# A hybrid encoder layer on one core: branch A's first four score tiles set between the last token tiles of its q projection

## The chip, the cores and the metric

The kernel runs on one core of a Trainium2 chip. The metric is device microseconds of one execution. Beside the times there is the trace of one profiled execution. Engines are named as the profile does: PE is TensorE (PEld its weight loads), DVE is VectorE, ACT is ScalarE, POOL is GpSimd, SP is SyncE, which issues nearly all DMAs here.

## The reference

One encoder layer on 1024 tokens of width 1024, in float32. Two attention branches share one projection, are merged by gates, and a squared-ReLU MLP and a gated embedding follow:

```python
h = rmsnorm(x, norm_mix_g[i])
z = h @ w_in[i]
qa, ka, va, qb, kb, vb, ga, gb = jnp.split(z, split_at, axis=-1)
y_a = mixer_a(qa, ka, va, q_norm_g[i], k_norm_g[i], row_ids, col_ids) @ w_out_a[i]
y_b = mixer_b(qb, kb, vb, rel_bias) @ w_out_b[i]
x = x + (gate_a * y_a + gate_b * y_b) @ w_out[i]
x = x + jnp.square(jax.nn.relu(rmsnorm(x, norm_mlp_g[i]) @ w_ff1[i])) @ w_ff2[i]
x = x + sigmoid(rmsnorm(x, norm_ple_g[i]) @ w_ple_gate[i]) * (p[i] @ w_ple[i])
return rmsnorm(x, final_norm_g)
```

Branch A (`mixer_a`) is dense attention of 8 q heads on 2 k/v heads of width 128. q and k are RMS-normed per head and turned by a rotary table; the softmax runs over all 1024 keys.

## The kernel before, in words

Every float32 product is made of three products of rounded halves: `split` writes `hi` (ACT, L235) and `lo = src - hi` (DVE, L236), and `mm3` (all its matmuls at L239) multiplies hi by hi, hi by lo and lo by hi. Memory is handed out by regions (`Region`), stacks that grow from the left and the right end of SBUF. When a region is closed, a later one may take its addresses, and the framework then sets the waits that this needs. Within the two `tc.manual_schedule` blocks PE runs in program order. Everything else, and the order on ACT, DVE, POOL and SP, is put in order by the framework's scheduler.

The change lies between the stages of branch A:

- `qkv_a` projects k and v (block 0) and q (blocks 1 and 2, four heads each), each block in eight token tiles of 24 matmuls. A tile is squared and summed on ACT (L861) and turned by the rotary table on DVE (L814, L819, L821). Two tiles later PE transposes it (`turn`, L835), ACT copies it out of PSUM (L840) and SP stores it to `qd`. The two last turns of block 2 are left over in `self.turns`. `load_q` brings one q head back and splits it (tile `rq`).
- `attend_a` runs 16 units (head, half of the tokens). A unit has four score tiles (`scores`: 6 matmuls into two PSUM banks, the row maximum on DVE at L926, its product with the row's scale at L928, the exponential on ACT at L930), then 8 key chunks of transposed weights (`weights`: four transposes at L936 and a split, tile `rp`) and their products with v (`values`, 6 matmuls for two chunks). The loop sets the scores of unit u beside the weights and values of unit u-1. `finish` ends a unit: it copies the result (L950), takes reciprocals of the denominators (L952), stores them to DRAM and loads them back as a row spread over all partitions (`rd`, `rb`), multiplies (L957) and splits into `oA` (tile `ro`, L235 and L236).
- `merged_b` (after unit 1's scores are set) splits the merged result of branch B into `oB` (tile `ro` as well).
- `mix_outputs` follows. Its first products need the out-projection's weights, split into the ring `wt` of region `rwt` (8 slots of 1024 words): per column block `wa` (hi, lo) and `wb` (one slot for both).

PSUM has eight banks of 512 words. In `qkv_a` the projection rings over banks 4 to 7, the turns over banks 2 and 3. In `attend_a` the scores take the pairs 0, 1 and 2, 3, the weights' transposes banks 4 to 6, the values bank 7.

The left stack during attention holds, in this order and in words per partition: `kv` 8192, `rq0` 2048, `fp1` 4096, `rq1` 2048, `fp0` 4096, `fp` 3104. Region `fa` (2560: `mix` and the two q rotary tables) is closed when `qkv_a` ends. Afterwards `m` (8192), `rwt` (8192) and `wo` (8192) stand at the same left end.

Of the kernel before, what the change touches and what calls it, by code (L numbers as in the profile page):

```python
# [10 lines left out]
F32 = mybir.dt.float32  # L11
F32R = mybir.dt.float32r
# [8 lines left out]
NT = S // P  # L21
KD = D // P
GRID_W = 64
HA, HKV, DA = 8, 2, 128
# [52 lines left out]
class Ring:  # L77
# [3 lines left out]
    def next(self):  # L81
        s = self.slots[self.i % len(self.slots)]
        self.i += 1
        return s
# [22 lines left out]
def v3(ap, k):  # L107
    return ap.rearrange("p (k c) -> p k c", k=k)
# [117 lines left out]
class Layer:  # L226
# [112 lines left out]
    def mix_inputs(self):  # L339
        tc, nc, io = self.tc, self.nc, self.io  # L340
        rh = Region(tc, "rh", F32R, "right")
        hT = [v3(rh.take(8192), KD) for _ in range(2)]
        wt = rh.ring(N_WT, 1024)
        w_in = io["w_in"][0]
# [239 lines left out]
        self.p_late = [self.fp1.take(1024) for _ in range(4)]  # L584
        halves = [a[:, o:o + 512] for a in self.p_late for o in (0, 512)]
        t_ring, stage = Ring(halves[:6]), Ring(halves[6:])
        fa = Region(tc, "fa", F32, "left")
        mix = fa.take(512)
        tabs = [v3(fa.take(1024), NT) for _ in range(2)] + tabs
        beside = self.merge_b(qk[0], Ring([qk[1][:, :S]] + u_ring.slots))  # L590
        with tc.manual_schedule(engines={mybir.EngineType.PE}):
            self.qkv_a(w_in, wt, hT, tabs, gtmp, t_ring, stage, lambda: self.weights_b(mix), beside)
            fa.close()
            fm.close()
            fq.close()
            rh.close()
            self.attend_a()

    def bias_rows(self, tmp, st, ps):

# [219 lines left out]
                                in1=sin[:, a:a + 32].unsqueeze(1).to_broadcast([P, n, 32]), op=ALU.mult)  # L820
        v.tensor_tensor(out=t1[:, :w], in0=t1[:, :w], in1=t2[:, :w], op=ALU.add)  # L821

    def qkv_a(self, w_in, wt, hT, tabs, gtmp, t_ring, stage, after_kv, beside):

        nc = self.nc
        ps_a, ps_t = Ring(self.bank[4:]), Ring(self.bank[2:4])
        self.ps_w = self.bank[1]
        q_tabs = self.rope_tables("q_norm_g", tabs[:2], gtmp, nc.vector)
        self.turns = []

        def turn(blk, t, t1, n):
            sl = slice(t * P, (t + 1) * P)
            pp = ps_t.next()[:, :n * P]
            for h in range(n):
                nc.tensor.transpose(pp[:, h * P:(h + 1) * P], t1[:, h * P:(h + 1) * P], self.ident)  # L835
            if blk == 0:
                self.split(self.kT[0][:, :, sl], self.kT[1][:, :, sl], v3(pp, 2))
            else:
                st, h0 = stage.next(), (blk - 1) * 4
                nc.scalar.activation(st, pp, AF.Copy)  # L840
                self.load(self.dr["qd"][h0:h0 + 4, :, sl].rearrange("h p t -> p h t"), v3(st, 4))

        for blk in range(3):
            c0 = (C_KA, C_QA, C_QA + 512)[blk]
            w = []
            for kk in range(4):
                w += self.w_rows(w_in, 2 * kk, c0, 512, wt)
            for t in range(NT):
                sl = slice(t * P, (t + 1) * P)
                ps = ps_a.next()  # L850
                for k in range(KD):
                    self.mm3([ps], (hT[0][:, k, sl], hT[1][:, k, sl]), [w[k]], k == 0, k == KD - 1)
                if len(self.turns) == 2:
                    self.turns.pop(0)()
                t1, t2 = t_ring.next(), t_ring.next()
                n = 2 if blk == 0 else 4
                tc_, ts_ = (tabs[2], tabs[3]) if blk == 0 else (tabs[0], tabs[1])
                sm = self.small.next()
                for h in range(n):
                    ss = sm[:, h:h + 1] if blk == 0 else self.q_scale(self.qss, 4 * blk - 4 + h, t)  # L860
                    nc.scalar.activation(t2[:, h * P:(h + 1) * P], ps[:, h * P:(h + 1) * P], AF.Square, accum_out=ss)  # L861
                if blk == 0:
                    self.split(self.vA[0][:, t, :], self.vA[1][:, t, :], ps[:, 256:512])
                self.rope(ps[:, :n * P], n, tc_[:, t, :], ts_[:, t, :], t1, t2)
                if blk == 0:
                    xe, y, tt = sm[:, 2:4], sm[:, 4:6], sm[:, 6:8]
                    nc.vector.tensor_scalar(xe, sm[:, 0:2], 1.0 / DA, EPS, op0=ALU.mult, op1=ALU.add)
                    self.rsqrt(y, xe, tt)
                    for h in range(2):
                        nc.vector.tensor_scalar(t1[:, h * P:(h + 1) * P], t1[:, h * P:(h + 1) * P],  # L870
                                                y[:, h:h + 1], None, op0=ALU.mult)
                self.turns.append(lambda a=(blk, t, t1, n): turn(*a))
                if blk == 0 and t >= NT - 2:
                    next(q_tabs)
                if blk == 1 and t == 2:
                    after_kv()
                if blk == 1 and t >= 4 or blk == 2 and t < 2:
                    next(beside)
                if blk == 2 and t == 3:
                    self.load_q(0)  # L880
            if blk:
                x, r, tt = (a[:, 32 * blk - 32:32 * blk] for a in (self.qss, self.rq, self.qtmp))
                nc.vector.tensor_scalar(x, x, 1.0 / DA, EPS, op0=ALU.mult, op1=ALU.add)
                self.rsqrt(r, x, tt)
                nc.vector.tensor_scalar(r, r, DA ** -0.5, None, op0=ALU.mult)
# [9 lines left out]
        self.split(q[0], q[1], raw)  # L895


    def attend_a(self):
        tc, nc = self.tc, self.nc
        self.ro = Region(tc, "ro", F32R, "right")  # L900
        self.oA = [v3(self.ro.take(8192), HA) for _ in range(2)]
        self.oB = [v3(self.ro.take(2048), 2) for _ in range(2)]
        rp = Region(tc, "rp", F32R, "right")
        pt_ring = rp.ring(6, 1024)
        self.rq_pools.append(Region(tc, "rq1", F32R, "left"))
        self.qr.append([self.rq_pools[1].take(1024) for _ in range(2)])
        f0, fp = (Region(tc, n, F32, "left") for n in ("fp0", "fp"))
        p_ring = Ring([f0.take(1024) for _ in range(4)] + self.p_late)
        ou_ring, rb_ring = fp.ring(3, 512), fp.ring(3, 512)
        den_ring = fp.ring(4, 8)  # L910
        s_ps, t_ps, o_ps = Ring(self.bank2[:2]), Ring(self.bank[4:7]), Ring(self.bank[7:])

        def scores(u, j):
            h, half = divmod(u, 2)
            if half == 0 and j == 0 and h:
                self.load_q(h)
            q = self.qr[h % 2]
            kv = h // (HA // HKV)
            t = half * 4 + j
            sl = slice(t * P, (t + 1) * P)  # L920
            ps = s_ps.next()
            self.mm3([ps[:, 0:512], ps[:, 512:1024]], (q[0][:, sl], q[1][:, sl]),
                     [tuple(self.kT[i][:, kv, c * 512:(c + 1) * 512] for i in range(2)) for c in range(2)],
                     True, True)
            nm = self.small.next()[:, 0:1]
            nc.vector.tensor_reduce(out=nm, in_=ps, axis=AX.X, op=ALU.max, negate=True)  # L926
            r = self.q_scale(self.rq, h, t)
            nc.vector.tensor_tensor(out=nm, in0=nm, in1=r, op=ALU.mult)  # L928
            p = p_ring.next()
            nc.scalar.activation(p, ps, AF.Exp, bias=nm, scale=r, accum_out=dens[u][:, j:j + 1])  # L930
            return p

        def weights(u, probs, kc, o):
            pp = t_ps.next()
            for j in range(4):
                nc.tensor.transpose(pp[:, j * P:(j + 1) * P], probs[j][:, kc * P:(kc + 1) * P], self.ident)  # L936
            pt = pt_ring.next()
            pt = (pt[:, 0:512], pt[:, 512:1024])
            self.split(pt[0], pt[1], pp)
            return u, pt, kc, o  # L940
# [19 lines left out]

        nu = 2 * HA
        dens = {u: None for u in range(nu)}
        probs, late = None, []

        def flush():
            while late:
                args = late.pop(0)
                values(*args)
                if args[2] == NT - 1:
                    finish(args[0], args[3])  # L970

        for u in range(nu + 1):
            nxt = []
            if u < nu:
                dens[u] = den_ring.next()
            for j in range(4):
                if u < nu:
                    nxt.append(scores(u, j))
                if self.turns:
                    self.turns.pop(0)()  # L980
                if u > 0:
                    if j == 0:
                        o = o_ps.next()
                    new = [weights(u - 1, probs, kc, o) for kc in (2 * j, 2 * j + 1)]
                    flush()
                    late += new
            probs = nxt
            if u == 1:
                self.merged_b()
        flush()  # L990
        for region in (rp, fp, f0, self.rq_pools[1], self.fp1, self.rq_pools[0], self.kv):
            region.close()

    def merged_b(self):
# [378 lines left out]
```

## Time and profile before

| | us |
|---|---|
| median of 3 runs | 1803.49 |
| lowest, highest | 1802.71, 1805.03 |
| the profiled execution | 1805.11 |
| its span in the trace | 1803.3 |
| PE busy | 1742.9 |
| DVE busy | 1244.7 |
| ACT busy | 796.4 |

The profiled execution takes 1.8 us more than its span, and 1.62 us more than the median. Times in the trace count from the span's start. `[0.88 <-ACT fp L840]` behind a row means that the engine sat idle for 0.88 us before it and that ACT's instruction at line 840, which handles tile `fp`, ended that. In a row merged from several instructions the second number runs from the first start to the last end. PEclk is the granted clock of TensorE as a share of full speed.

### The profile page before, as it was taken

The page shows a single profiled execution, that of the slowest core. Times are in us where ns is not written, and L with a number is a line of the kernel's source. Part 1 is how long each engine was busy: PE and PEld are TensorE (multiplying, and loading weights), DVE is VectorE, ACT ScalarE, POOL GpSimd, SP SyncE. Part 2 cuts the span into 40 slices and gives each one's busy share as a digit, 9 for nine tenths or more (in the row PEclk, how much of TensorE's full clock was granted, in tenths as well). Part 3 has the DMA queues.
Part 4 walks back from the last instruction along what each step waited for, and adds up shares of the span by engine and source line. Part 5 has one row for each costly group of instructions (what it writes and reads, how often), then busy time and mean ns, then how long its engine had stood idle before and what let it go on. Part 6 is the DMA issues. An engine that isn't in the chain of part 4 may idle for free.

```text
span 1803.3 us, 22775 instructions
## 1 busy us (share of the span) xinstructions
PE 1742.9 (97%) x8451; PEld 1439.7 (80%) x8451; DVE 1244.7 (69%) x2070; ACT 796.4 (44%) x1383; POOL 420.5 (23%) x234
## 2 busy tenths in 40 slices
PE   6999999999998999999999999999999999989897
PEld 5888888877887888888888778888888888867786
DVE  7556754476765787875455686555569999999564
ACT  6333233266333677774333354443546333332331
POOL 0242322000000000000000134343337666672000
PEclk9999999999999999999999999999999999999999
DMA  6243234475163222225432223333353333331111
GB/s 216 74 154 138 94 117 152 154 230 168 36 180 110 64 42 24 31 24 167 160 129 94 94 82 109 126 105 112 142 207 135 117 116 112 123 128 35 36 38 45
DMA packets 132287, 199.20 MB, mean 110 GB/s; under 512 B 25508, under 2 KB 92932, under 8 KB 132176
## 3 DMA queue, kind: packets, MB, share of 16 engines
q1 hardware_dynamic: 131008, 194.17, 34.0%
q0 software_dynamic: 1168, 3.57, 0.7%
q8 instruction: 67, 1.10, 0.3%
q14 instruction: 44, 0.36, 0.1%
HBM read 146.12 MB, written 54.73 MB: 111 GB/s over the span
## 4 chain that ended last, share of the span: by engine, by line
PE 59%; DVE 7%; issue 1%; ACT 0%; DMA 0%; DVEq 0%; ACTq 0%
PE psum L239 55%; PE psum L936 3%; DVE rc L236 3%; DVE facc L1206 2%; DVE hb L236 0%; PE psum L275 0%; PE psum L1062 0%; DVE fsum L1227 0%; DVE rg L236 0%; ACT fp L930 0%; ACT rc L235 0%; DVE base L926 0%; PE psum L1294 0%; DMA base<-in_p 0%; ACT hb L235 0%
## 5 line engine op out<-in xcount | busy, mean ns | idle before, releaser
L239 PE MATMUL psum<-rc,rc 128*128 128x512 f32 x1464 | 342.2, 394 | 10.4 <-DVE rc L236 9.6
L239 PE MATMUL psum<-rh,rh 128*128 128x512 f32 (+1 forms) x1428 | 335.8, 389 | 1.6 <-ACT rh L235 1.1
L239 PEld LDWEIGHTS psum<-rc,rc 128*128 128x128 f32 x1464 | 277.8, 190 | 71.3 <-DVE rc L236 10.4
L239 PEld LDWEIGHTS psum<-rh,rh 128*128 128x128 f32 x1428 | 260.9, 190 | 59.3 <-issue 5.9
L151 POOL TENSOR_TENSOR base<-base 128x512 f32<-128x512 f32 x17 | 29.0, 1703 | 770.7 <-DMA base<-in_w_ff 604.9
L239 PE MATMUL psum<-ht,rh 128*128 128x512 f32 x624 | 145.7, 389 | 0.0
L239 PE MATMUL psum<-hc,rc 128*128 128x512 f32 x576 | 137.9, 389 | 0.0
L239 PEld LDWEIGHTS psum<-ht,rh 128*128 128x128 f32 x624 | 117.2, 188 | 24.3
L235 ACT ACTIVATE rh<-base 128x512 fp32r<-128x512 f32 (+1 forms) x77 | 61.2, 808 | 147.4 <-PE psum L239 120.2
L239 PEld LDWEIGHTS psum<-hc,rc 128*128 128x128 f32 x576 | 108.1, 188 | 22.4
L236 DVE TENSOR_TENSOR rh<-base,rh 128x512 fp32r<-128x512 f32 (+1 forms) x77 | 78.3, 1027 | 62.8 <-PE psum L239 39.0
L235 ACT ACTIVATE rc<-base 128x1024 fp32r<-128x1024 f32 (+1 forms) x64 | 51.5, 827 | 151.5 <-PE psum L239 147.6
L239 PE MATMUL psum<-ro,rwt 128*128 128x512 f32 x480 | 109.0, 389 | 0.0
L239 PEld LDWEIGHTS psum<-ro,rwt 128*128 128x128 f32 x480 | 90.1, 188 | 18.7
L209 DVE TENSOR_TENSOR fw<-fw,psum 128x512 f32<-128x512 f32 x91 | 74.3, 817 | 42.4 <-PE psum L239 41.4
L239 PE MATMUL psum<-rp,kv 128*128 128x512 f32 x384 | 103.5, 405 | 0.0
L926 DVE TENSOR_REDUCE base<-psum 128x1 f32<-128x1024 f32 x64 | 78.3, 1224 | 36.3 <-PE psum L239 36.3
L239 PE MATMUL psum<-kv,rq 128*128 128x512 f32 x384 | 100.3, 398 | 1.6 <-ACT fp L840 0.9
L1206 DVE TENSOR_TENSOR facc<-facc,psum 128x1024 f32<-128x1024 f32 x84 | 98.5, 1207 | 0.0
L239 PE MATMUL psum<-hb,rc 128*128 128x512 f32 x384 | 93.8, 394 | 4.5 <-DVE hb L236 4.5
L236 DVE TENSOR_TENSOR rc<-fsum,rc 128x1024 fp32r<-128x1024 f32 x56 | 94.2, 1711 | 3.3 <-ACT rc L235 3.3
L236 DVE TENSOR_TENSOR rc<-rfb,rc 128x512 fp32r<-128x512 f32 (+1 forms) x62 | 74.1, 1212 | 31.3 <-ACT rc L235 31.0
(273 smaller groups left out, 3036.2 us busy)
## 6 DMA issues: line engine op xcount, KB each, us to landing
base<-in_w_ff SPq DMA_DIRECT2D x20, 1024.0 KB, 5.5
base<-in_w_in SPq DMA_DIRECT2D x13, 1024.0 KB, 5.3
s_u<-rfa SPq DMA_DIRECT2D x22, 512.0 KB, 2.6
base<-in_w_in SPq DMA_DIRECT2D x20, 512.0 KB, 4.8
fg<-s_gd SPq DMA_DIRECT2D x16, 512.0 KB, 5.8
rfa<-s_u SPq DMA_DIRECT2D x8, 1024.0 KB, 4.9
fraw<-in_w_ff SPq DMA_DIRECT2D x8, 1024.0 KB, 5.8
s_gd<-fw SPq DMA_DIRECT2D x14, 512.0 KB, 3.0
```

The lines of the kernel that those rows point to most:

```text
L151: g.tensor_tensor(out=s1, in0=a21, in1=a22, op=ALU.add)
L209: self.nc.vector.tensor_tensor(out=self.c[out], in0=self.c[a], in1=self.p[i], op=op)
L235: self.nc.scalar.activation(hi, src, AF.Copy)
L236: (eng or self.nc.vector).tensor_tensor(out=lo, in0=src, in1=hi.bitcast(F32), op=ALU.subtract)
L239: self.nc.tensor.matmul(out, lhsT=lhsT, rhs=rhs, start=start, stop=stop)
L926: nc.vector.tensor_reduce(out=nm, in_=ps, axis=AX.X, op=ALU.max, negate=True)
L936: nc.tensor.transpose(pp[:, j * P:(j + 1) * P], probs[j][:, kc * P:(kc + 1) * P], self.ident)
L1206: v.tensor_tensor(out=o, in0=o, in1=ps, op=ALU.add)
```

## The change

The generator `attend_a` is now made before the projection and advanced from within it. Its first advance, at tile 3 of the last q block, closes the three regions of branch B and opens its own. The advances at tiles 4 to 7 each emit one score tile of unit 0. After the projection the generator goes on with unit 1's loop, and with it come the two turns left over. For this the turns of `qkv_a` keep one PSUM bank (4) in place of two, and the projection has three (5 to 7) in place of four. `load_q(0)` comes one tile earlier. Region `fa` stays open to the end of attention: its five halves serve as the three slots of `ou_ring` and two of the three of `rb_ring`, so that `fp` shrinks from 3104 to 544 words.

```diff
-        fa = Region(tc, "fa", F32, "left")
-        mix = fa.take(512)
-        tabs = [v3(fa.take(1024), NT) for _ in range(2)] + tabs
+        self.fa = Region(tc, "fa", F32, "left")
+        mix = self.fa.take(512)
+        q_tabs = [self.fa.take(1024) for _ in range(2)]
+        tabs = [v3(a, NT) for a in q_tabs] + tabs
+        self.fa_halves = [a[:, o:o + 512] for a in q_tabs for o in (0, 512)] + [mix]
         beside = self.merge_b(qk[0], Ring([qk[1][:, :S]] + u_ring.slots))
+        attend = self.attend_a((fm, fq), rh)
         with tc.manual_schedule(engines={mybir.EngineType.PE}):
-            self.qkv_a(w_in, wt, hT, tabs, gtmp, t_ring, stage, lambda: self.weights_b(mix), beside)
-            fa.close()
-            fm.close()
-            fq.close()
-            rh.close()
-            self.attend_a()
+            self.qkv_a(w_in, wt, hT, tabs, gtmp, t_ring, stage, lambda: self.weights_b(mix), beside, attend)
+            for _ in attend:
+                pass
...
-        ps_a, ps_t = Ring(self.bank[4:]), Ring(self.bank[2:4])
-        self.ps_w = self.bank[1]
+        ps_a, ps_t = Ring(self.bank[5:]), Ring(self.bank[4:5])
+        self.ps_w = self.bank[3]
...
-                if blk == 2 and t == 3:
+                if blk == 2 and t == 2:
                     self.load_q(0)
+                if blk == 2 and t > 2:
+                    next(attend)
...
-        ou_ring, rb_ring = fp.ring(3, 512), fp.ring(3, 512)
+        ou_ring, rb_ring = Ring(self.fa_halves[:3]), Ring(self.fa_halves[3:] + [fp.take(512)])
...
-        probs, late = None, []
+        probs, late = [], []
+        dens[0] = den_ring.next()
+        for j in range(4):
+            yield
+            probs.append(scores(0, j))
+        yield
+        rh.close()
+        self.ro = Region(tc, "ro", F32R, "right")
...
-        for u in range(nu + 1):
+        for u in range(1, nu + 1):
...
-        for region in (rp, fp, f0, self.rq_pools[1], self.fp1, self.rq_pools[0], self.kv):
+        for region in (rp, fp, f0, self.rq_pools[1], self.fa, self.fp1, self.rq_pools[0], self.kv):
             region.close()
```

Where it moves instructions is best seen in three places. The first is PE after the last projection tile. `kv,rq` is a score tile, `base,fp` at L835 a turn (fp11, fp12, fp13 for tiles 5, 6 and 7), L936 the transposes of the weights. Before:

```order
L835 MATMUL psum1_85<-base1_58,fp11_3159 128x128 x4
L239 MATMUL psum1_85<-kv1_3147,rq01_3154 128x512 x2
L239 MATMUL psum1_85<-kv2_3148,rq01_3154 128x512 x2
L239 MATMUL psum1_85<-kv1_3147,rq02_3155 128x512 x2
L835 MATMUL psum1_85<-base1_58,fp12_3160 128x128 x4
L239 MATMUL psum1_85<-kv1_3147,rq01_3154 128x512 x2
L239 MATMUL psum1_85<-kv2_3148,rq01_3154 128x512 x2
L239 MATMUL psum1_85<-kv1_3147,rq02_3155 128x512 x2
L835 MATMUL psum1_85<-base1_58,fp13_3161 128x128 x4
```

And of the change:

```order
L835 MATMUL psum1_85<-base1_58,fp11_3159 128x128 x4
L239 MATMUL psum1_85<-kv1_3147,rq01_3154 128x512 x2
L239 MATMUL psum1_85<-kv2_3148,rq01_3154 128x512 x2
L239 MATMUL psum1_85<-kv1_3147,rq02_3155 128x512 x2
L239 MATMUL psum1_85<-kv1_3147,rq01_3154 128x512 x2
L239 MATMUL psum1_85<-kv2_3148,rq01_3154 128x512 x2
L239 MATMUL psum1_85<-kv1_3147,rq02_3155 128x512 x2
L835 MATMUL psum1_85<-base1_58,fp12_3160 128x128 x4
L936 MATMUL psum1_85<-base1_58,fp01_4176 128x128
L936 MATMUL psum1_85<-base1_58,fp02_4177 128x128
L936 MATMUL psum1_85<-base1_58,fp03_4178 128x128
L936 MATMUL psum1_85<-base1_58,fp04_4179 128x128
```

The score tiles in the second piece are the last of unit 0 and the first of unit 1; three score tiles of unit 0 now stand further up, each behind one of the turns of tiles 2, 3 and 4, and the turn of tile 6 is followed at once by the weights of unit 0.

The second place is ACT behind the squares of the last tile (fp13 at L861), of the change:

```order
L861 ACTIVATE fp13_3161,base12_73<-psum1_85 128x128 x2
L235 ACTIVATE ro3_4400<-base14_75 128x1024 x2
L840 ACTIVATE fp14_3162<-psum1_85 128x512
L930 ACTIVATE fp04_4179,fp2_4181<-psum1_85,base2_63,base11_72 128x1024
L235 ACTIVATE rp1_4405<-psum1_85 128x512
L235 ACTIVATE rp2_4406<-psum1_85 128x512
L930 ACTIVATE fp11_3159,fp3_4182<-psum1_85,base3_64,base11_72 128x1024
L840 ACTIVATE fp14_3162<-psum1_85 128x512
```

Here one exponential of unit 0 (fp04) is left after the last tile, where four stood before; the splits of branch B (`ro3`) are still here, and the copy of the last turn (the second L840) stands behind unit 1's first exponential.

The third place is ACT at the end of attention. L950 is the copy of unit 15's result, `ro1` the split of its product, `rwt1` and `rwt3` the first out-projection weights (`wa` and `wb` of column block 0). Before:

```order
L235 ACTIVATE rp1_4350<-psum1_85 128x512
L235 ACTIVATE rp2_4351<-psum1_85 128x512
L235 ACTIVATE rwt1_6326<-base14_75 128x1024
L235 ACTIVATE rwt3_6328<-base14_75 128x256
L235 ACTIVATE rwt4_6329<-base14_75 128x1024
L235 ACTIVATE rwt6_6331<-base14_75 128x256
L950 ACTIVATE fp1_4371<-psum1_85 128x512
L235 ACTIVATE ro1_4343<-fp1_4371 128x512
```

And of the change:

```order
L235 ACTIVATE rp1_4405<-psum1_85 128x512
L235 ACTIVATE rp2_4406<-psum1_85 128x512
L950 ACTIVATE fa2_3167<-psum1_85 128x512
L235 ACTIVATE ro1_4398<-fa2_3167 128x512
L235 ACTIVATE rwt1_6321<-base14_75 128x1024
L235 ACTIVATE rwt3_6323<-base14_75 128x256
```

The four weight splits that stood ahead of unit 15's finish now stand behind it. On DVE `rwt2` and the lower half of `rwt3` likewise come behind the product L957 and `ro2` of unit 15. On PE the first product behind the last values is one matmul on `rwt1`, then the twelve on `rwt3`.

## Rows read from the trace of the kernel before

**Rows 1.** The page's first part: busy time and share of each engine.
```profile
PE 1742.9 (97%) x8451; PEld 1439.7 (80%) x8451; DVE 1244.7 (69%) x2070; ACT 796.4 (44%) x1383; POOL 420.5 (23%) x234
```
**Rows 2.** Windows: length, busy PE, PEld, DVE, ACT, POOL; granted clock; DMA share; GB/s.
```profile
577.00:600.00 23.00, 16.82 (x74) 13.01 (x73) 17.13 (x39) 14.21 (x29) 0.00 (x0) 0.85 0.35 104
600.00:700.00 100.00, 100.00 (x556) 85.28 (x555) 81.08 (x134) 76.60 (x129) 0.00 (x0) 1.00 0.26 36
...
586.40:591.70 5.30, 5.28 (x15) 4.32 (x16) 3.76 (x11) 0.60 (x1) 0.00 (x0) 0.50 0.38 131
...
1615.90:1619.20 3.30, 3.30 (x8) 2.65 (x9) 3.30 (x3) 0.34 (x1) 3.30 (x2) 0.50 0.00 0
...
1032.90:1038.90 6.00, 6.00 (x18) 5.06 (x19) 4.26 (x3) 4.57 (x4) 1.79 (x1) 0.50 0.26 87
```
**Rows 3.** Timeline of PE, end of the projection: start, length, instruction, [idle before].
```profile
571.59 5.71 PE L239 MATMUL psum<-rh,rh 128*128 128x512 f32 x24
577.14 0.60 PE L835 MATMUL psum<-base,fp 128*128 128x128 f32 x4
577.49 1.64 PE L239 MATMUL psum<-kv,rq 128*128 128x512 f32 x6
578.97 0.60 PE L835 MATMUL psum<-base,fp 128*128 128x128 f32 x4
580.45 1.65 PE L239 MATMUL psum<-kv,rq 128*128 128x512 f32 x6 [0.88 <-ACT fp L840]
586.42 1.11 PE L835 MATMUL psum<-base,fp 128*128 128x128 f32 x4 [4.31 <-ACT fp L930]
587.18 5.16 PE L239 MATMUL psum<-kv,rq 128*128 128x512 f32 x12
...
603.17 1.53 PE L239 MATMUL psum<-kv,rq 128*128 128x512 f32 x6
...
606.79 1.53 PE L239 MATMUL psum<-kv,rq 128*128 128x512 f32 x6
```
**Rows 4.** Timeline of DVE, the same stretch.
```profile
580.48 1.22 DVE L926 TENSOR_REDUCE base<-psum 128x1 f32<-128x1024 f32 x1
...
583.59 1.22 DVE L236 TENSOR_TENSOR ro<-base,ro 128x1024 fp32r<-128x1024 f32 x1
```
**Rows 5.** Timeline of ACT, the same stretch.
```profile
578.83 1.08 ACT L235 ACTIVATE ro<-base 128x1024 fp32r<-128x1024 f32 x1
579.78 0.62 ACT L840 ACTIVATE fp<-psum 128x512 f32<-128x512 f32 x1
...
582.49 1.20 ACT L930 ACTIVATE fp<-psum,base,base 128x1024 f32<-128x1024 f32 x1 [0.19 <-DVE base L928]
```
**Rows 6.** Timeline of PE, end of attention and first out-projection products.
```profile
817.74 2.98 PE L239 MATMUL psum<-rp,kv 128*128 128x512 f32 x12
820.56 39.83 PE L239 MATMUL psum<-ro,rwt 128*128 128x512 f32 x175
```
**Rows 7.** Timeline of ACT, the same stretch.
```profile
818.56 2.62 ACT L235 ACTIVATE rwt<-base 128x1024 fp32r<-128x1024 f32 x4
...
826.18 0.63 ACT L235 ACTIVATE ro<-fp 128x512 fp32r<-128x512 f32 x1 [4.52 <-DVE fp L957]
```
**Rows 8.** Timeline of DVE, the same stretch.
```profile
825.46 0.69 DVE L957 TENSOR_TENSOR fp<-fp,fp 128x512 f32<-128x512 f32 x1 [3.10 <-DMA fp<-s_rd]
...
826.85 0.69 DVE L236 TENSOR_TENSOR ro<-fp,ro 128x512 fp32r<-128x512 f32 x1 [0.36 <-ACT ro L235]
```
**Rows 9.** Timeline of SP's DMA issues towards the end of attention.
```profile
752.97 0.38 SPq L232 DMA_DIRECT2D base<-in_w_out_b  x1
...
810.54 1.75 SPq L232 DMA_DIRECT2D s_rd<-fp  x4
820.05 0.32 SPq L232 DMA_DIRECT2D fp<-s_rd  x1
```
**Rows 10.** The tile view of `s_rd`: all its transfers, from issue to landing.
```profile
DMA to landing us min/median/max: 4.0/7.5/8.6
```

More of the change, by code (lines that the diff above doesn't have):

```diff
@@ L821, in rope, with qkv_a @@
         v.tensor_tensor(out=t1[:, :w], in0=t1[:, :w], in1=t2[:, :w], op=ALU.add)
-    def qkv_a(self, w_in, wt, hT, tabs, gtmp, t_ring, stage, after_kv, beside):
+    def qkv_a(self, w_in, wt, hT, tabs, gtmp, t_ring, stage, after_kv, beside, attend):
         nc = self.nc
-        ps_a, ps_t = Ring(self.bank[4:]), Ring(self.bank[2:4])
-        self.ps_w = self.bank[1]
+        ps_a, ps_t = Ring(self.bank[5:]), Ring(self.bank[4:5])
+        self.ps_w = self.bank[3]
         q_tabs = self.rope_tables("q_norm_g", tabs[:2], gtmp, nc.vector)
@@ L895, in load_q, with attend_a @@
         self.split(q[0], q[1], raw)
-    def attend_a(self):
+    def attend_a(self, done, rh):
         tc, nc = self.tc, self.nc
[L900 to L904, printed above, removed]
+        for region in done:
+            region.close()
         self.rq_pools.append(Region(tc, "rq1", F32R, "left"))
@@ L962, in attend_a @@
         dens = {u: None for u in range(nu)}
-        probs, late = None, []
+        probs, late = [], []
[6 more added lines that the diff above has]
+        self.ro = Region(tc, "ro", F32R, "right")
+        self.oA = [v3(self.ro.take(8192), HA) for _ in range(2)]
+        self.oB = [v3(self.ro.take(2048), 2) for _ in range(2)]
+        rp = Region(tc, "rp", F32R, "right")
+        pt_ring = rp.ring(6, 1024)
         def flush():
@@ L980, in attend_a @@
                     self.turns.pop(0)()
[L981 to L986, printed above, removed]
+                if j == 0:
+                    o = o_ps.next()
+                new = [weights(u - 1, probs, kc, o) for kc in (2 * j, 2 * j + 1)]
+                flush()
+                late += new
             probs = nxt
```

## The prediction

> **What bounds the kernel now.** I read the page first: PE is busy for 1742.9 us, 97% of the span [rows 1], so only what moves PE can move the time. Then I read windows around the change. In steady attention PE is busy for the whole of 100 us, while at the passage from projection to attention 23.00 us hold 16.82 us of PE work [rows 2], so 6.2 us are idle. The timeline of PE names the waits: the second score tile waits 0.88 us for the copy of a turn, and the last turn waits 4.31 us for an exponential [rows 3]. Both are conflicts over PSUM banks: the turns ring over banks 2 and 3, and so does every second score tile. After that wait the granted clock is 0.50, the lower of the two levels (1.2 GHz), from 586.40 to 591.70 [rows 2]; twelve score matmuls take 5.16 us there [rows 3], where two tiles 1.48 us apart would take about 3.1. So the passage loses 6.2 us to idling and half of those 5.30 us, 2.6, to the clock: 8.8 us in all. The last views are of the other end of attention, since region `fa` now lives until there: PE goes from the last values to the out-projection with no gap [rows 6].
>
> **Part 1, the passage into attention.** The count starts at the turn of tile 5, right behind the last projection tile: 577.14 before. Unit 2's first score tile starts at 606.79 [rows 3], 29.65 us later. Of the change I take the same stretch from the orders.
>
> Three of unit 0's score tiles now stand before that point. Each still costs PE its 1.48 us (577.49 to 578.97) [rows 3], together 4.4 us. Nothing should wait for them there: a projection tile lasts 5.71 us [rows 3], and in it DVE gains one maximum of 1.22 us and ACT one exponential of 1.20 [rows 4, 5].
>
> Then, from zero: turn 0.35, last score tile of unit 0 1.48, first of unit 1 1.48, turn of tile 6 0.35. PE is through these at 3.7 us and wants the weights of unit 0, which need the last exponential of unit 0. Its maximum takes the place on DVE that unit 0's first maximum had, 580.48 or 3.3 us, and that one's exponential began at 582.49 or 5.35 us [rows 4, 5], with some small steps between that now come later. I take 5.2, plus 1.2 for the exponential and 0.2 for reading its sum: 6.6 us. Only three of the four transposes of a chunk can run before. So PE is idle for some 2.5 us, in two pieces, where it lost 8.8. To 7.0 us go the other transposes, to 8.5 the next score tile, to 8.9 the turn of tile 7, to 9.3 one chunk. The next chunk uses bank 4, which that turn has just filled; the copy that frees it stands on ACT behind unit 1's first exponential, whose maximum waits its turn on DVE beside a split of branch B (1.22 us) [rows 4]. I put its end at 9.8, so 0.5 us more are lost. Four transposes and two chunks of values bring 11.7, two rounds of 3.62 us (603.17 to 606.79) [rows 3] 18.9. The second of those splits falls into unit 1 as well; I allow 0.3 for it: 19.2. With the 4.4 us in front this is 23.6 us against 29.65: **a gain of 6.0 us**. Its bounds: 8.8, if no new wait remains; 3.4, if the clock falls here too and costs the same 2.6 as now.
>
> **Part 2, PSUM and the small moves.** One turn bank instead of two, three projection banks instead of four: a bank of turns is wanted again only a projection tile later, 5.71 us [rows 3], and its copy takes 0.62 [rows 5], so I price this at nothing. If that cover failed, each of 24 tiles could lose its copy. Head 1's split, drawn out of the passage, is inside part 1.
>
> **Part 3, the end of attention.** This term follows from `fa` staying open. The out-projection's ring `rwt` takes 8192 words from `rq0` on. Before, these were `rq0`, `fp1` and `rq1`; now they are `rq0`, `fp1` and 2048 words of `fa`, which hold the `ou` and `rb` slots of the last `finish`. A region seems to be taken over as a whole: the source of the first `wb` was asked for at 752.97 [rows 9], the slot of `wa` is memory of `rq0`, idle since head 6, and still the first four splits run only at 818.56, behind the last weights of unit 15 [rows 7]. In the order of the change ACT's `rwt1` and `rwt3` stand behind `ro1` of unit 15; `rwt1` waits for DVE too, so presumably for `ro2`, the last reader of `ou`.
>
> That finish is late because of its round trip through DRAM. The reciprocals go out at 810.54, the row is asked for at 820.05 [rows 9], and L957 starts at 825.46 after waiting 3.10 us for it [rows 8]. Before, this held up nothing that PE wanted soon. Now: `ro1` to 826.81 [rows 7], `ro2` to 827.54 [rows 8], then `rwt1` and `rwt3`, half of four splits that took 2.62 us [rows 7]: to 828.85. PE used `rwt3` at 820.56 [rows 6] and now can at 828.9; one matmul on `rwt1`, 0.25 us, runs ahead. **A stall of 8.1 us**; 7.3, if `rwt1` does not wait for `ro2`.
>
> After such a gap the clock is low. PE worked at 0.50 for 5.30, 3.30 and 6.00 us after three gaps of this trace [rows 2], and each costs half of itself, 1.6 to 3.0 us; I take 2.3. PE has no idle time behind this stall [rows 6], so nothing absorbs it. **A loss of 10.4 us**, between 8.9 and 11.1.
>
> **A rule weighed.** One small transfer of the round trip takes 4.0 to 8.6 us from issue to landing, 7.5 in the middle [rows 10]. The Trainium skill (DMA: Bandwidth & Descriptors, the anatomy of one DMA) states a nearly constant cost of about 2 us per transfer, measured on the gpsimd path; by an estimate from that page the row would be back before PE ends, and the sum would come out as in the second rival. The trace has durations for these very transfers and they are longer, so the sum uses them.
>
> **Sum.** 1805.11 - 6.0 + 10.4 = 1809.5 for an execution like the profiled one, whose span of 1803.3 has 1.8 us around it that the change leaves alone. That execution stood 1.62 us above the median, so the median goes to **1807.9 us**, 4.4 us or 0.24% slower. A measurement of this kernel can tell some 0.2%, 3.6 us, from no change.
>
> **The rivals.**
> *The end costs nothing (faster).* If the first weights were covered, the gain would stand alone: 1803.5 - 6.0 = 1797.5. For it speaks that the ring's first slots share no address with `ou`. Against it stands ACT's fixed order: `rwt1` cannot run before `ro1`, and `ro1` needs the row that came at 825.46 [rows 8]. It decides if that row lands before about 817. Chance 0.06.
> *The round trip is short.* With both transfers at the least landing, 4.0 us [rows 10], the row is there by about 820.3, and the chain hangs on the last values, which end at 820.72 [rows 6]: their copy 0.6, L957 0.69, `ro1` 0.63, `ro2` 0.69, two weight splits 1.31 [rows 7, 8], to 824.7. Stall 3.9, clock 2.3, gain 6.0: +0.2, 1803.7. Against it: 9.5 us lie between the issues of store and load [rows 9]. Chance 0.07.
> *The clock falls at the passage too.* The new gaps there are split, but close together. Then the gain is 3.4 and the result 1803.5 + 7.0 = 1810.5. Chance 0.17.
> *Both terms at their kind ends.* `rwt1` not held by `ro2`, the clock back early (7.3 + 1.6), the gain 7, between 6.0 and its bound: +1.9, 1805.4. Chance 0.18.
> *The change does not do what it says.* Head 0 of q comes back late for its first score tile, or the single turn bank holds PE up. Then part 1 gains nothing: 1803.5 + 10.4 = 1813.9. Chance 0.04.
> The forecast itself has 0.48.
>
> **How the numbers follow.** The forecast with its own spread, 1806.5 to 1809.7, lies mostly above 1807.1, which is 0.2% more than now: of 0.48 about 0.44, with 0.17 and 0.04, give 0.65 for slower. The kind ends, most of the short round trip and the rest of the forecast give 0.28 for no change, the first rival and a little of the second 0.07 for faster. The range, 1804.5 to 1811.5, leaves out the first rival, the second and the last, 0.17.
>
> **What would show it.** Right: on PE's timeline a wait of about 8 us between the last values and the first product on `rwt`, ended by ACT `rwt` L235, then a window at clock 0.50; at the passage waits of 2 to 3 us in all in front of L936, and unit 2's first scores some 19 us after the turn of tile 5. Wrong: no wait before the products on `rwt`, or ACT's `rwt` splits ahead of L957; or waits inside the q projection.

## The result, and the profile after

The changed kernel takes 1816.65 us (median of 4 runs, 1812.98 to 1821.23) against 1803.1 for the kernel before beside it: ratio 1.0075 [1.0056, 1.0094], slower by more than the interval leaves open. 1807.9 was forecast, 1804.5 to 1811.5 the range: the sign is right, but the change costs 13.5 us and not 4.4. The profiled execution took 1817.44 with a span of 1815.6, 12.3 more than before.

PE's busy time is 1.5 us above what it was ([rows 1]: 1742.9), so 10.8 of the 12.3 us are idle time. The page's first part:

```profile
PE 1744.4 (96%) x8451; PEld 1439.9 (79%) x8451; DVE 1245.1 (69%) x2070; ACT 796.4 (44%) x1383; POOL 420.4 (23%) x234
```

**The passage came out as forecast.** The timeline of PE (start, length, instruction, [idle before]), the answer to [rows 3], and a window (length, busy PE, PEld, DVE, ACT, POOL; granted clock; DMA share; GB/s):

```profile
579.51 0.60 PE L835 MATMUL psum<-base,fp 128*128 128x128 f32 x4
...
584.06 0.55 PE L936 MATMUL psum<-base,fp 128*128 128x128 f32 x3 [0.74 <-ACT fp L840]
586.04 0.77 PE L936 MATMUL psum<-base,fp 128*128 128x128 f32 x5 [1.43 <-ACT fp L930]
...
589.30 0.66 PE L936 MATMUL psum<-base,fp 128*128 128x128 f32 x4 [0.25 <-ACT fp L840]
...
591.18 1.55 PE L239 MATMUL psum<-kv,rq 128*128 128x512 f32 x6
...
598.48 1.55 PE L239 MATMUL psum<-kv,rq 128*128 128x512 f32 x6
```
```profile
579.51:598.48 18.97, 16.55 (x94) 13.56 (x93) 16.35 (x38) 14.95 (x30) 0.00 (x0) 1.00 0.40 125
```

From the turn of tile 5 to unit 2's first scores it is 18.97 us (19.2 forecast), with 2.4 us of waits in front of L936 and the clock at 1.00. With the 4.4 us of the three score tiles that went ahead, 23.4 stand against 29.65: a gain of 6.2.

**It is lost again in unit 2, where the prediction did not look.** PE's timeline goes on:

```profile
605.91 1.55 PE L239 MATMUL psum<-kv,rq 128*128 128x512 f32 x6
607.30 0.60 PE L936 MATMUL psum<-base,fp 128*128 128x128 f32 x4
613.57 1.12 PE L936 MATMUL psum<-base,fp 128*128 128x128 f32 x4 [5.67 <-DVE rp L236]
614.33 2.91 PE L239 MATMUL psum<-rp,kv 128*128 128x512 f32 x6
617.04 2.22 PE L239 MATMUL psum<-kv,rq 128*128 128x512 f32 x6
...
621.36 1.53 PE L239 MATMUL psum<-kv,rq 128*128 128x512 f32 x6
```

PE waits 5.67 us for a split of the weights and then works at the lower clock. From the third score tile of unit 2 (605.91) to the first of unit 3 (621.36) 15.45 us pass, where two rounds of unit 1 take 7.3 (591.18 to 598.48): 8.1 us lost. The windows split it into 5.67 us of idling and 45% of 5.43 us at a granted clock of 0.55, 2.4. (The last window belongs to the end of attention.)

```profile
607.90:613.57 5.67, 0.00 (x1) 0.01 (x1) 1.42 (x4) 0.70 (x2) 0.00 (x0) 0.83 0.44 88
613.57:619.00 5.43, 5.43 (x16) 4.47 (x17) 3.53 (x6) 3.39 (x6) 0.00 (x0) 0.55 0.18 6
...
828.77:834.20 5.43, 5.43 (x14) 4.39 (x15) 2.43 (x3) 5.40 (x7) 0.00 (x0) 0.56 0.61 189
```

Why the split is late, DVE's timeline tells. L952 is the reciprocal of unit 0's denominators, L957 the product that needs their row back from DRAM:

```profile
595.48 0.17 DVE L952 RECIPROCAL fp<-fp 128x4 f32<-128x4 f32 x1
...
603.85 1.22 DVE L926 TENSOR_REDUCE base<-psum 128x1 f32<-128x1024 f32 x1 [1.14 <-PE psum L239]
612.15 0.69 DVE L957 TENSOR_TENSOR fa<-fa,fa 128x512 f32<-128x512 f32 x1 [7.07 <-DMA fa<-s_rd]
...
612.83 1.28 DVE L236 TENSOR_TENSOR rp<-psum,rp 128x512 fp32r<-128x512 f32 x2
```

and the same two instructions before:

```profile
595.29 0.18 DVE L952 RECIPROCAL fp<-fp 128x4 f32<-128x4 f32 x1 [1.42 <-ACT fp L930]
```
```profile
613.10 0.68 DVE L957 TENSOR_TENSOR fp<-fp,fp 128x512 f32<-128x512 f32 x1
```

The attention runs some 8 us earlier now (unit 2's first scores at 598.48 for 606.79), but the reciprocal does not: 595.48 for 595.29. Before, it went as soon as its exponential was done ([1.42 <-ACT fp L930]); now the exponential is done at 585.98, and the reciprocal stands in DVE's order behind the splits and small steps of the passage. ACT's last row of that exponential, and a window over the 9.50 us up to the reciprocal, in which DVE is busy for 9.38:

```profile
585.79 0.19 ACT L930 ACTIVATION_READ_ACCUMULATOR fp<-psum,base,base 128x1 f32 x1
```
```profile
585.98:595.48 9.50, 9.19 (x52) 7.73 (x53) 9.38 (x23) 6.84 (x13) 0.00 (x0) 1.00 0.50 170
```

L957 keeps its place among unit 2's instructions. So 17.8 us lay between the two before, and now DVE reaches L957 at 605.08, after 9.6. SP's timeline gives the row's way, its stores and its load, now and before:

```profile
595.68 4.07 SPq L232 DMA_DIRECT2D s_rd<-fp  x4
...
607.58 0.32 SPq L232 DMA_DIRECT2D fa<-s_rd  x1
```
```profile
595.49 1.75 SPq L232 DMA_DIRECT2D s_rd<-fp  x4
604.65 0.32 SPq L232 DMA_DIRECT2D fp<-s_rd  x1
```

The row is there at 612.1, 16.6 us after the reciprocal. In these 7.07 us the trace shows DVE start nothing, and the split that PE wants stands behind L957. Part of the 7.07 us is the row's way itself: from the reciprocal to the load's issue it is 12.1 us now and was 9.4, so by an estimate from these rows some 2.7 of them. Why the way was longer was not tried.

**The end of attention stalls as forecast.** PE's, ACT's and DVE's timelines; the answers to [rows 6 to 8]:

```profile
817.84 2.98 PE L239 MATMUL psum<-rp,kv 128*128 128x512 f32 x12
828.77 41.51 PE L239 MATMUL psum<-ro,rwt 128*128 128x512 f32 x172 [7.95 <-ACT rwt L235]
```
```profile
826.27 0.63 ACT L235 ACTIVATE ro<-fa 128x512 fp32r<-128x512 f32 x1 [4.82 <-DVE fa L957]
827.66 1.36 ACT L235 ACTIVATE rwt<-base 128x1024 fp32r<-128x1024 f32 x2 [0.76 <-DVE ro L236]
```
```profile
825.54 0.69 DVE L957 TENSOR_TENSOR fa<-fa,fa 128x512 f32<-128x512 f32 x1 [5.94 <-DMA fa<-s_rd]
```

From the start of the last values to the first product on `rwt` it is 10.93 us where it was 2.82: 8.1. The clock of 0.56 behind it costs 44% of 5.43 us, 2.4. Together 10.5.

**The account** is then -6.2 + 8.1 + 10.5 = +12.4, and the span grew by 12.3. That the two agree to 0.1 us is luck, because two stretches that no term covers cancel: the turn of tile 5 comes 2.4 us later than before with 4.4 us more work ahead of it, so 2.0 were gained there, 1.6 of them ahead of the projection (the same transposes of branch B start at 422.20 for 423.81), and 1.7 were lost behind the third gap of [rows 2], whose first products come 10.6 us later (1043.46 for 1032.89).

### The profile page after: what moved, and what is told of

It is laid out like the page before. It is cut to its first block, busy times and chain, and to the rows that moved or that the text cites. A ratio compares the mean times of both kernels' runs of the same rounds, so it can differ in the third digit from the quotient of the medians.

```text
span 1815.6 us, 22773 instructions
## 1 busy us (share of the span) xinstructions
PE 1744.4 (96%) x8451; PEld 1439.9 (79%) x8451; DVE 1245.1 (69%) x2070; ACT 796.4 (44%) x1383; POOL 420.4 (23%) x234
## 4 chain that ended last, share of the span: by engine, by line
PE 56%; DVE 15%; issue 2%; DMA 2%; ACT 1%; SPq 0%; DVEq 0%; ACTq 0%
PE psum L239 52%; DVE rc L236 7%; DVE facc L1216 5%; PE psum L936 3%; DMA s_rd<-fp 1%; DVE fsum L1237 1%; DMA fa<-s_rd 1%; DVE rg L236 1%; DVE hb L236 0%; PE psum L835 0%; PE psum L275 0%; PE psum L1072 0%; DVE base L926 0%; DVE fsum L1262 0%; DVE rp L236 0%
## 5 line engine op out<-in xcount | busy, mean ns | idle before, releaser
L239 PEld LDWEIGHTS psum<-rc,rc 128*128 128x128 f32 x1464 | 278.2, 191 | 72.5 <-DVE rc L236 10.3
```

What stands on the lines that cost most here:

```text
L239: self.nc.tensor.matmul(out, lhsT=lhsT, rhs=rhs, start=start, stop=stop)
```

## The experiments

Two theories had to be told apart. **Theory A:** two stalls that have nothing to do with each other, one from the place of the `rwt` ring, one from the late reciprocal in front of an in-order queue. **Its rivals:** the end's wait is the last unit's own; the row is late through SP and the DMA; interleaving costs something itself; a wait taken away comes back in the next unit. The table has every run; the time before is that of the kernel before on the same chip. The changed kernel has no run beside the experiments, so what an edit gives back is the difference of two distances to the kernel before, and runs of one kernel lie 3 to 9 us apart.

| run | edit | us | before | ratio [95%] |
|---|---|---|---|---|
| the changed kernel | | 1816.65 | 1803.10 | 1.0075 [1.0056, 1.0094] |
| e1 | ring off the broadcast rings, operands moved 128 B | 1829.75 | 1804.32 | 1.0143 [1.0129, 1.0157] |
| e2 | reciprocals early | 1810.92 | 1804.32 | 1.0036 [1.0022, 1.0049] |
| e3 | e1 and e2 | 1819.61 | 1804.32 | 1.0085 [1.0071, 1.0098] |
| e4 | before, ring on the broadcast rings | 1816.54 | 1804.32 | 1.0063 [1.0051, 1.0076] |
| e5 | before, reciprocals early | 1804.55 | 1804.00 | 1.0000 [0.9991, 1.0009] |
| e6 | e3, no move of operands | 1809.22 | 1804.00 | 1.0027 [1.0014, 1.0040] |
| e7, 128 | changed kernel, operands moved 128 B | 1839.21 | 1804.00 | 1.0194 [1.0180, 1.0208] |
| e7, 256 | changed kernel, operands moved 256 B | 1818.88 (1 run) | 1804.00 | |
| e8 | e3, operands moved 256 B | 1799.46 | 1803.82 | 0.9976 [0.9967, 0.9985] |
| e10 | e1, operands moved 256 B | 1806.54 | 1803.82 | 1.0027 [1.0015, 1.0038] |
| e9 | e8, branch B's splits later | 1802.70 | 1803.82 | 0.9993 [0.9984, 1.0003] |

**e1, the ring taken off the broadcast rings.** `wo` takes `rwt`'s place, `rwt` stands behind it with seven slots, the sums' ring goes to the base region.

```diff
+        self.den_ring = base.ring(4, 8)
...
-        mix = self.fa.take(512)
...
+        self.fx0 = Region(tc, "fmix", F32, "left")
+        mix = self.fx0.take(512)
...
-        den_ring = fp.ring(4, 8)
+        den_ring = self.den_ring
...
-        rm, rwt, wo0 = (Region(tc, n, d, "left") for n, d in (("m", F32), ("rwt", F32R), ("wo", F32R)))
+        rm, wo0, rwt = (Region(tc, n, d, "left") for n, d in (("m", F32), ("wo", F32R), ("rwt", F32R)))
...
-        wt = rwt.ring(8, 1024)
+        wt = rwt.ring(7, 1024)
```

> The changed kernel, with the routing weights' ring moved so that it no longer lies on the space of the attention's two broadcast rings (ou, rb). Theory A (the end of the attention waits because this ring's tiles stand on space that the last finish still reads): the 7.95 us wait before the first routing product falls to 1 us or less and the stretch at clock 0.50 behind it goes, so about 10.6 us less than the changed kernel, near 1806; the 5.67 us wait in unit 2 stays. Rival (the wait at the end comes from the last unit's chain itself, wherever the ring lies): 7 us or more of wait stay, and the time stays within 2 us of the changed kernel's.

The wait at the end is gone (no `rwt` wait is left on PE), the one in unit 2 stays (7.6 us), and the time rose by 13 us. Neither theory said that. PE's busy time is 1763.7, 19 us more: products of unchanged shape take longer, for a reason that e7 shows. e1 is judged by e10, its like without that flaw.

**e7, the operands' addresses alone.** One unused piece in the base region moves everything behind it by 128 or 256 bytes per partition.

```diff
         self.qtmp = base.take(64)
+        base.take(32)
```

> The changed kernel with 128 unused bytes per partition added to the base region, nothing else. Address theory: the products of the first stage (ht by rh) and of the last stages (hc by rc) go from 389 to 395 ns, 12 to 18 us more than the changed kernel. Rival (e1 and e3 were slow for another reason): 389 ns, time within 2 us of the changed kernel.

> As the run before, with 256 bytes. Address theory, fine form (it is the place within 256 bytes that counts): 389 ns as in the changed kernel. Coarse form (any shift counts): 395 ns or another value above 389.

The groups of PE (count | busy us, mean ns | idle before) by 128 bytes, and by 256:

```profile
L239 PE MATMUL psum<-ht,rh 128*128 128x512 f32 x624 | 149.6, 395 | 0.0
L239 PE MATMUL psum<-hc,rc 128*128 128x512 f32 x576 | 141.0, 394 | 0.0
```
```profile
L239 PE MATMUL psum<-ht,rh 128*128 128x512 f32 x624 | 145.7, 389 | 0.0
L239 PE MATMUL psum<-hc,rc 128*128 128x512 f32 x576 | 137.9, 389 | 0.0
```

389 ns is also what the changed kernel has. The move by 128 bytes costs 22 us, somewhat more than expected, the move by 256 next to nothing (one run, 2.2 us above the median). So e1 and e3 carry a cost of their own; measured against e7 with 128 bytes, e1 is 0.5% faster, 9 us.

**e10, the first edit alone without that flaw** (`base.ring(4, 16)`).

> The first edit alone (the routing weights' ring off the broadcast rings), with 256 bytes as in e8. Theory A: about 10.6 us less than the changed kernel, 1805 to 1807; the wait in unit 2 stays at 5 us or more. Rival (the two stalls are not independent): over 1810 or under 1802.

1806.54, 2.7 above the kernel before where the changed kernel is 13.5 above: 10.8 us back, 10.6 expected. The nearness is in part luck: the nine runs lie between 1805.43 and 1813.00, four of them above 1809. The trace decides. PE's timeline keeps the stall in unit 2 and has none at the end:

```profile
613.86 1.12 PE L938 MATMUL psum<-base,fp 128*128 128x128 f32 x4 [5.40 <-DVE rp L236]
```
```profile
818.34 3.01 PE L239 MATMUL psum<-rp,kv 128*128 128x512 f32 x12
821.19 29.18 PE L239 MATMUL psum<-ro,rwt 128*128 128x512 f32 x128
```

**e4, the first cause put into the kernel before.** Region `fp`, with both broadcast rings, is opened ahead of `rq1`, so that `rwt` lands on it.

```diff
+        fp = Region(tc, "fp", F32, "left")
...
-        f0, fp = (Region(tc, n, F32, "left") for n in ("fp0", "fp"))
+        f0 = Region(tc, "fp0", F32, "left")
...
-        for region in (rp, fp, f0, self.rq_pools[1], self.fp1, self.rq_pools[0], self.kv):
+        for region in (rp, f0, self.rq_pools[1], fp, self.fp1, self.rq_pools[0], self.kv):
```

> The kernel before, order of the work kept, with its regions opened in another order so that the routing weights' ring lies on the two broadcast rings as it does in the changed kernel. Theory A: a wait of about 8 us before the first routing product, half clock behind it, and about 10.6 us more than the kernel before, near 1814. Rival (the overlap of the rings costs nothing unless the units run in the changed order): no wait over 1 us there, time within 2 us of the kernel before.

12.2 us more, with no score tile moved; 10.6 were expected. PE's timeline has the same wait:

```profile
818.62 2.98 PE L239 MATMUL psum<-rp,kv 128*128 128x512 f32 x12
830.11 40.19 PE L239 MATMUL psum<-ro,rwt 128*128 128x512 f32 x170 [8.51 <-ACT rwt L235]
```

From the last values to the first product it is 11.5 us for 2.8 at [rows 6], 8.7 lost, and the clock behind it (0.64 for 4.09 us) costs 1.5. The other 2 us of the 12.2 were not traced. With e10 the first cause is shown from both sides: the place of the ring makes the stall, the interleaving does not.

**e2, the second cause taken away.** The reciprocals and their stores are written right behind the unit's last exponential; `finish` only loads the row.

```diff
+            if j == 3:
+                rden = dens[u][:, 4:8]
+                nc.vector.reciprocal(rden, dens[u][:, 0:4])
+                for i in range(4):
+                    self.load(self.dr["rd"][u, i], rden[:, i:i + 1])
...
-            rden = dens[u][:, 4:8]
-            nc.vector.reciprocal(rden, dens[u][:, 0:4])
-            for j in range(4):
-                self.load(self.dr["rd"][u, j], rden[:, j:j + 1])
```

> The changed kernel, with each unit's reciprocal and the stores of its rows given out right behind the last exponential of the unit's scores, instead of with the finish; the re-laid rings stay. Theory A (unit 0's reciprocal stands behind VectorE's backlog of the passage, so its row comes back late and heads VectorE's queue in unit 2): the 5.67 us wait in unit 2 and the half clock behind it go, unit 3's first scores start about 8 us earlier than in the changed kernel, and the time is about 8.4 us less, near 1808; the wait of about 8 us at the end of the attention stays. Rival (the row is late because its stores share SyncE's queue and the DMA with the q heads' loads): the reciprocal runs near 586 us, yet the row lands no earlier than 610, the wait keeps 4 us or more, and the time is within 3 us of the changed kernel's.

DVE's timeline (L933 is the reciprocal, L958 the product), then PE's:

```profile
588.34 0.17 DVE L933 RECIPROCAL fp<-fp 128x4 f32<-128x4 f32 x1
...
606.32 0.68 DVE L958 TENSOR_TENSOR fa<-fa,fa 128x512 f32<-128x512 f32 x1
```
```profile
580.85 0.60 PE L835 MATMUL psum<-base,fp 128*128 128x128 f32 x4
...
614.46 1.53 PE L239 MATMUL psum<-kv,rq 128*128 128x512 f32 x6
```

The product no longer waits, and neither does PE. From the turn of tile 5 to unit 3's first scores it is 33.61 us, where the changed kernel takes 41.85 (579.51 to 621.36): 8.2 us, as the theory says. In the median 6.6 above the kernel before remain of 13.5, so 6.9 came back, 8.4 expected; the stall at the end (8.3 us) is still there. The rival falls: SP's queue is still slow, the load goes out 10.4 us after the stores (588.88 and 599.27), but with the earlier start the row is there when DVE comes to it. The longer way of the row had its share in the changed kernel's wait (2.7 us, above), but the place of the reciprocal alone takes the whole wait away.

**e5, the same edit in the kernel before.**

> The kernel before with the early reciprocals and stores alone, no re-laid rings, no moved score tiles. Theory A (the late reciprocal costs only where the score tiles stand early): no change, within 2 us of the kernel before. Rival (early reciprocals are a gain of their own, whatever the order): 4 us or more faster.

1.0000 [0.9991, 1.0009]: no gain of its own. There the reciprocal was never in the way.

**e3 and e6, both edits together, twice spoilt.** e3 has the slower products of e1.

> Both edits together. Theory A (two stalls, independent of each other): both waits go, about 19 us less than the changed kernel, 1797 to 1798, some 6 us under the kernel before. Rival 1 (putting the score tiles between the projection's tiles costs time of its own, by the single turn bank or by slower matmuls): the time stays at 1803 or above, with no wait over 3 us in units 1 to 3. Rival 2 (a wait taken away here only moves to the next unit): a new wait of 4 us or more in units 2 to 4, time 1802 or above.

It shows neither stall (the longest wait of PE in the attention is 1.4 us), and is 10 us better than e1 (15.3 above the kernel before for 25.4), so the second edit works on top of the first. What it missed by is the address: e8 below, which differs in the size of one small ring, is 19.7 us better. e6 leaves the sums' ring in region `fp`, so that no address moves:

```diff
-        self.den_ring = base.ring(4, 8)
...
-        den_ring = self.den_ring
+        den_ring = fp.ring(4, 8)
```

> Both edits as in e3, but the sums' ring stays where the changed kernel has it, so that nothing in the base region grows and no later tile's address moves by 128 bytes. Address theory (in e1 and e3 every operand behind the base region stood 128 bytes further, and the 128x512 products took 395 ns in place of 389): the products take 389 ns again as in the changed kernel, both waits stay away, and the time is 1796 to 1798, some 6.5 us under the kernel before. Rival (the slower products come from the re-ordered regions, or from the missing eighth slot): 395 ns stays, time near 1819.

The products are back at 389 ns, but the time is 1809.22. ACT's timeline and PE's show why:

```profile
815.91 1.06 ACT L235 ACTIVATE rwt<-base 128x1024 fp32r<-128x1024 f32 x1 [6.70 <-DMA s_rd<-fp]
816.88 1.06 ACT L235 ACTIVATE rp<-psum 128x512 fp32r<-128x512 f32 x2
```
```profile
818.89 1.12 PE L942 MATMUL psum<-base,fp 128*128 128x128 f32 x4 [6.78 <-DVE rp L236]
```

The first weight split now waits for the stores that read the last unit's reciprocals out of `fp`, and the last weights of unit 15 stand behind it on ACT. It is the first cause again with another reader. By the sizes `rwt`'s seven slots end where the sums' ring begins, so no address is shared: the wait is for the whole region, which is what the prediction had guessed from the kernel before.

**e8, both edits with 256 bytes.**

> Both edits as in e3, the sums' ring in the base region, but with 256 bytes in place of 128, so that the later operands keep their place within 256 bytes. Theory A: products of 389 ns, no wait over 3 us between the turn of tile 5 and the first routing product, and a time of 1796 to 1799, 5 to 8 us under the kernel before. Rival (with both stalls gone another one takes their place): a wait of 4 us or more in the attention or right behind it, time 1803 or above.

1799.46, 0.9976 [0.9967, 0.9985], faster than both kernels. PE's timeline at unit 1, and at the end of attention:

```profile
600.85 0.77 PE L943 MATMUL psum<-base,fp 128*128 128x128 f32 x5 [1.30 <-ACT fp L932]
```
```profile
812.18 2.98 PE L239 MATMUL psum<-rp,kv 128*128 128x512 f32 x12
815.01 35.30 PE L239 MATMUL psum<-ro,rwt 128*128 128x512 f32 x155
```

The first product on `rwt` starts 5.55 us earlier than at [rows 6]. The two edits give back 10.8 and 6.9 us alone and 17.9 together (13.5 above the kernel before to 4.4 below it): they add up, within the spread of the runs. The time lies 0.5 us over the expected range's top. One wait of 1.30 us is new in the stretch, and ACT's timeline shows what is behind it, an exponential that waits for a store of q:

```profile
599.50 1.20 ACT L932 ACTIVATE fp<-psum,base,base 128x1024 f32<-128x1024 f32 x1 [2.06 <-DMA s_qd<-fp]
```

By the end of the span 2.8 us of the 5.55 are gone, which stays open (below); the profiled execution is also the slowest of e8's ten (1802.28).

**e9, branch B's splits moved out of the passage.**

```diff
-            if u == 1:
+            if u == 14:
                 self.merged_b()
```

> As e8, with branch B's merged rows split into the output operand in the middle of the attention and no longer at its start, so that two 1 us activations leave ScalarE's queue, and two subtractions VectorE's, in the passage. Theory A's reading of the passage (its remaining waits of 0.7 and 1.4 us come from these queues' backlog): 1 to 2 us less wait in front of unit 0's first transposes, and 1 to 2 us less than e8. Rival (these waits are the score chain's own length): the waits and the time stay within 0.5 us of e8.

The three waits in the passage are the same to the hundredth (0.74, 1.43, 0.25), although the two splits are gone from ACT there. So theory A's reading of these waits falls as far as branch B's splits go. The exponential behind the 1.43 us is held by DVE:

```profile
583.63 0.69 DVE L816 TENSOR_TENSOR fp<-psum,fa 128x512 f32<-128x512 f32 x1 [3.98 <-ACT fp L863]
584.24 0.87 DVE L821 TENSOR_TENSOR fp<-psum,fa 128x128 f32<-128x128 f32 x4
585.03 1.21 DVE L928 TENSOR_REDUCE base<-psum 128x1 f32<-128x1024 f32 x1
```

The score tile is done at about 583.6 on PE (582.13 and six matmuls), and its maximum (L928) stands behind the rotary products of the last token tile. So DVE's queue has a part in the wait after all; an edit on that was not tried. And the splits found a worse place: ACT, and with it PE, wait for their row in the middle of the attention (in the profiled execution, the slowest of the twelve with 1807.57).

```profile
671.49 1.06 ACT L235 ACTIVATE ro<-base 128x1024 fp32r<-128x1024 f32 x1 [5.52 <-DMA base<-s_ob]
```
```profile
673.81 1.02 PE L943 MATMUL psum<-base,fp 128*128 128x128 f32 x4 [3.85 <-DVE rp L236]
```

The same thing again, after L957, e6 and the small wait in e8: an instruction that waits for a transfer, with work behind it on its engine that PE needs.

## Why the prediction was right and wrong

- **What bounds, and part 1:** right in mechanism and size. 18.97 us for 19.2, waits of 2.4 us for 3.0, no clock fall, gain 6.2 for 6.0. One cause is other than told: the first piece, 0.74 us, is ended by the copy of the turn of tile 6 and not by the exponential, since the turns now use a bank that the transposes want. It cost nothing more, as PE would have waited for the exponential, done at 585.98, in any case.
- **The step that failed:** part 1 ended its count at unit 2's first scores with "two rounds of 3.62 us" and took everything behind that as the steady state of before. The sum has no term for unit 0's `finish`, which the change pulls forward with the scores while its reciprocal stays. Put at nothing, that term measured +8.1 us in the trace of the changed kernel, and taking it away gave 8.2 us in the trace and 6.9 in the times (e2). The prediction priced exactly this chain, reciprocal, DRAM, L957, at unit 15, and did not ask whether it is in time at unit 0. No rival had it either, so the range ended below the result.
- **Part 2:** right. e8 keeps the single turn bank and the three projection banks; PE is busy there for the whole of 500 to 570 us, in the q projection, and no wait in the attention is over 1.43 us.
- **Part 3:** right. Stall 8.1 for 8.1, clock 2.4 for 2.3, together 10.5 for 10.4; undone in e10 (10.8) and put into the kernel before in e4 (12.2). [rows 6], from which the prediction took that nothing absorbs the stall, end at 860 us; the 10.6 us at 1043.46 show that nothing did up to there.
- **The rule weighed:** the transfers of `s_rd` land after 4.1, 7.3 and 10.3 us in the changed kernel (least, middle, longest), so the rows were the right price. By the estimate from the Trainium skill (DMA: Bandwidth & Descriptors, the anatomy of one DMA) of about 2 us each, which the page gives for the gpsimd path while these transfers are issued by SP, neither stall would have been this long; the runs do not bear it out for this round trip.
- **The rivals:** none came. The clock stayed at 1.00 through the passage, and the round trip was not short. What "the end costs nothing" would have given, had unit 2 cost nothing either, is e8: 4.4 us faster than before, 6.0 worked out.

What stays open: at equal places ahead of the change the kernels lie up to 3 us apart (e8 and e9 are alike there, and their turns of tile 5 come at 578.81 and 581.77), and behind 1040 us they drift by 1 to 3 us, with the wait for `hb` between 4.5 and 6.4 us. No edit was made on that, and the sums above leave it out.

## What to carry to other kernels

When work is pulled ahead, follow every chain that starts from it, not only the engine that gains: an instruction that waits for a DRAM round trip keeps its place in its engine's order, and is reached earlier, while the step that starts the trip may not move. Count the us between the trip's start and its use, before and after, for the first unit as well as for the last. And when a buffer's life is extended, look up which later region lands on it, and whose splits then stand behind its last reader.

## What was not expected of the hardware

In the two groups shown at e7, a product of 128x512 took 389 ns or 395 ns by the place of its operands alone: 128 bytes more in one region, and everything behind it, cost 22 us over the kernel, 256 bytes next to nothing (e7). Why was not tried. And the clock does not follow from a wait's length: behind the same waits of 0.74 and 1.43 us it stayed at 1.00 in e8 (585.30 to 588.70) and was 0.54 in e9 (588.30 to 591.90), and behind the 3.5 us gap at [rows 2], where PE had worked at 0.50 for 6.00 us, the changed kernel's next eight matmuls took 1.09 us where they had taken 1.97.
